# Sharing between two engines the scale that releases a store, and interleaving the tiles' rows in HBM, in a row-normalising kernel

## The chip, the cores and the metric

One core of one Trainium2 chip. The metric is device time in microseconds (us) of one execution.

## The reference

```python
x = np.random.randn(1024, 4096).astype(np.float32)      # eps = 1e-12
norm = np.sqrt(np.sum(x ** 2, axis=-1, keepdims=True) + eps)
return (x / norm).astype(np.float32)
```

16.78 MB are read, as many are written, and each element is squared once and scaled once.

## The kernel before

Two tiles of 128 partitions with four rows each. Both loads are issued at once; each store waits for all scales of its tile. Each row gets a sum of squares, a square root with a reciprocal (`norm`), and a scale.

```python
    def scale(self, r):                       # VectorE
        self.nc.vector.tensor_scalar_mul(
            out=self.x[:, r], in0=self.x[:, r], scalar1=self.rstd[:, r : r + 1])

    def scale_act(self, r):                   # ScalarE
        self.nc.scalar.activation(
            out=self.x[:, r], in_=self.x[:, r],
            func=ACT_F.Copy, scale=self.rstd[:, r : r + 1])
...
    x_t = x.rearrange("(t p r) d -> t p (r d)", p=P, r=R)           # P = 128, R = 4
    out_t = out_flat.rearrange("(t p r) d -> t p (r d)", p=P, r=R)
...
    for i, g in enumerate(groups):            # all loads are issued before this loop
        g.square_dve(R - 1)
        g.square_act(0); g.norm(0); g.scale(0)
        g.square_act(1); g.norm(1); g.norm(R - 1)
        g.scale(1); g.scale(R - 1)
        g.square_act(2); g.norm(2)
        if i < n_tiles - 1:
            g.scale_act(2)                    # the last scale of the first tile
        else:
            g.scale(2)
        store = nc.sync.dma_start(out=out_t[i], in_=g.flat())
```

## Time and profile before

| | before |
|---|---|
| time, median of the first 3 runs | 82.42 us (82.16 to 82.43) |
| profiled span | 80.7 us |
| DMA engines busy | 97.0% of the span |
| ScalarE, VectorE busy | 37%, 33% |
| loads landed at | 21.87 and 41.23 us |
| stores issued at | 39.21 and 56.61 us |
| stores landed at | 60.78 and 80.15 us |

The rows on landings and issues say it in short: four transfers of 8.39 MB follow each other at about 19.3 us apiece, and the compute lies beside them. The first store's own waits are in the view of the waits of the DMA queue's issuer (who waits, for what, us in total, times, longest; SPq is the queue of SyncE, which issues the DMAs, ACT is ScalarE and DVE is VectorE):

```profile
SPq L213 <- DMA xt<-in_x_dram: 22.4, 2, 20.7
SPq L213 <- ACT xt L69: 17.3, 1, 17.3
SPq L213 <- DVE xt L64: 15.3, 1, 15.3
```

The 17.3 us are the first store's wait for ScalarE's scale (L69) after the first load had landed. The last row, 15.3 us, is the second store's wait for VectorE's scale; it ends 3.4 us before the first engine has room for that store.

### The profile page before, as it was taken

The numbers are of one execution on the slowest core, as the hardware profiler recorded it, in microseconds if no ns is written. First come the engines' busy times: TensorE is split into PE (matmuls) and PEld (weight loads), VectorE is DVE, ScalarE is ACT, GpSimd is POOL, SyncE is SP. The second block draws the span as 40 slices with busy tenths as digits, with TensorE's granted clock in tenths as the row PEclk, the third lists the DMA queues.
The fourth block names the chain that finished last, engine by engine and source line by source line (L and its number), as shares of the span: only waits on it lengthen the run. The fifth ranks groups of instructions, "written<-read, shape, count | busy, mean of one in ns | idle before, by whom it ended". The sixth has DMA issues, their size and how long they took to land.

```text
span 80.7 us, 93 instructions
## 1 busy us (share of the span) xinstructions
DVE 26.2 (33%) x20; ACT 30.1 (37%) x23; POOL 0.2 (0%) x4
## 2 busy tenths in 40 slices
DVE  0000000000199599920059986999000000000000
ACT  6000000000199999989459999930000000000000
POOL 0000000000000000000000000000000000000000
DMA  9099998299998299998399992999993999993990
GB/s 520 0 520 520 520 520 390 130 520 520 520 520 390 130 520 520 520 520 390 130 520 520 520 520 130 390 520 520 520 520 130 390 520 520 520 520 130 390 520 0
DMA packets 576, 33.55 MB, mean 416 GB/s; under 512 B 64, under 2 KB 64, under 8 KB 64
## 3 DMA queue, kind: packets, MB, share of 16 engines
q1 hardware_dynamic: 576, 33.55, 97.0%
HBM read 16.78 MB, written 16.78 MB: 416 GB/s over the span
## 4 chain that ended last, share of the span: by engine, by line
DMA 50%; ACT 10%; DVE 9%; issue 0%
DMA xt<-in_x_dram 50%; ACT sq_act L33 9%; DVE xt L64 9%; ACT rstd L53 1%; DVE rstd L59 0%
## 5 line engine op out<-in xcount | busy, mean ns | idle before, releaser
L33 ACT ACTIVATE sq_act<-xt 128x4096 f32<-128x4096 f32 x6 | 21.6, 3608 | 21.9 <-DMA xt<-in_x_dram 21.9
L42 DVE SCALAR_TENSOR_TENSOR sq_dve<-xt 128x4096 f32<-128x4096 f32 x2 | 8.8, 4425 | 26.8 <-DMA xt<-in_x_dram 26.8
L64 DVE TENSOR_SCALAR xt<-xt,rstd 128x4096 f32<-128x4096 f32 x7 | 16.5, 2353 | 0.2
L69 ACT ACTIVATE xt<-xt,rstd 128x4096 f32<-128x4096 f32 x1 | 3.7, 3708 | 0.2 <-DVE rstd L59 0.2
L53 ACT ACTIVATE rstd<-ssq,eps_t 128x1 f32<-128x1 f32 x8 | 2.1, 288 | 0.1
L59 DVE RECIPROCAL rstd<-rstd 128x1 f32<-128x1 f32 x8 | 1.3, 159 | 2.4 <-ACT rstd L53 2.4
L33 ACT ACT_TABLE_LOAD x1 | 1.3, 1283 | 0.8 <-PEq L231 0.8
L53 ACT ACT_TABLE_LOAD x1 | 1.3, 1283 | 0.0
L33 ACT ACTIVATION_READ_ACCUMULATOR sq_act<-xt 128x1 f32 x6 | 1.1, 185 | 0.0
L184 DVE MEMSET eps_t<- 128x1 f32 x1 | 0.1, 59 | 0.9 <-PEq L231 0.9
L42 DVE DVE_READ_ACCUMULATOR sq_dve<-xt 128x1 f32 x2 | 0.2, 82 | 0.0
L231 POOL MEMSET const-bfloat16-1.0<- 128x1 bf16 x1 | 0.1, 101 | 0.0
L231 POOL MEMSET const-uint8-127<- 128x1 uint8 x1 | 0.1, 101 | 0.0
L231 POOL MEMSET const-float32-0.0<- 128x1 f32 x1 | 0.1, 98 | 0.2 <-issue 0.2
L231 POOL MEMSET const-float32-1.0<- 128x1 f32 x1 | 0.1, 98 | 0.0
## 6 DMA issues: line engine op xcount, KB each, us to landing
xt<-in_x_dram SPq DMA_DIRECT2D x2, 31.2
out_dram<-xt SPq DMA_DIRECT2D x2, 22.6
```

What stands on the lines that cost most here:

```text
L33: self.nc.scalar.activation(out=sq_a, in_=self.x[:, r], func=ACT_F.Square, accum_out=self.ssq[:, r : r + 1],)
L42: self.nc.vector.scalar_tensor_tensor(out=sq_v, in0=self.x[:, r], scalar=1.0, in1=self.x[:, r], op0=ALU.mult, op1=ALU.mult, accum_out=self ...
L53: self.nc.scalar.activation(out=self.rstd[:, r : r + n], in_=self.ssq[:, r : r + n], func=ACT_F.Sqrt, bias=self.eps_t,)
L59: self.nc.vector.reciprocal(out=self.rstd[:, r : r + n], in_=self.rstd[:, r : r + n])
L64: self.nc.vector.tensor_scalar_mul(out=self.x[:, r], in0=self.x[:, r], scalar1=self.rstd[:, r : r + 1])
L69: self.nc.scalar.activation(out=self.x[:, r], in_=self.x[:, r], func=ACT_F.Copy, scale=self.rstd[:, r : r + 1],)
L184: nc.vector.memset(eps_t, eps)
L231: nc = _bacc.Bacc("TRN2", target_bir_lowering=False, num_devices=1)
```

## The change

The intent is to release the first store sooner and to change how the tiles lie in HBM. ScalarE keeps 3072 of the 4096 elements of that scale and VectorE, idle at that time, takes 1024. Partition p of tile t now holds chunk 2p+t of four rows, so that the chunks of neighbouring partitions in one tile start 128 KiB apart in HBM instead of 64.

```diff
-    def scale_act(self, r):
+    def scale_by_both(self, r):
+        cut = 3 * self.D // 4
+        rstd = self.rstd[:, r : r + 1]
         self.nc.scalar.activation(
-            out=self.x[:, r], in_=self.x[:, r], func=ACT_F.Copy,
-            scale=self.rstd[:, r : r + 1])
+            out=self.x[:, r, :cut], in_=self.x[:, r, :cut], func=ACT_F.Copy,
+            scale=rstd)
+        self.nc.vector.tensor_scalar_mul(
+            out=self.x[:, r, cut:], in0=self.x[:, r, cut:], scalar1=rstd)
...
-    x_t = x.rearrange("(t p r) d -> t p (r d)", p=P, r=R)
-    out_t = out_flat.rearrange("(t p r) d -> t p (r d)", p=P, r=R)
+    x_t = x.rearrange("(p t r) d -> t p (r d)", t=n_tiles, r=R)
+    out_t = out_flat.rearrange("(p t r) d -> t p (r d)", t=n_tiles, r=R)
...
-            g.scale_act(2)
+            g.scale_by_both(2)
```

More of the change, by code (lines that the diff above doesn't have):

```diff
@@ L66, in scale @@
         )
-    def scale_act(self, r):
+    def scale_by_both(self, r):
+        cut = 3 * self.D // 4
+        rstd = self.rstd[:, r : r + 1]
         self.nc.scalar.activation(
-            out=self.x[:, r],
-            in_=self.x[:, r],
+            out=self.x[:, r, :cut],
+            in_=self.x[:, r, :cut],
             func=ACT_F.Copy,
-            scale=self.rstd[:, r : r + 1],
+            scale=rstd,
+        )
+        self.nc.vector.tensor_scalar_mul(
+            out=self.x[:, r, cut:], in0=self.x[:, r, cut:], scalar1=rstd
         )
```

## The prediction

> **What bounds the kernel now.** I began with the page of the profile: the busy shares, then the slices of DMA, then the chain.
>
> ```profile
> DVE 26.2 (33%) x20; ACT 30.1 (37%) x23; POOL 0.2 (0%) x4
> ...
> DMA  9099998299998299998399992999993999993990
> ...
> DMA packets 576, 33.55 MB, mean 416 GB/s; under 512 B 64, under 2 KB 64, under 8 KB 64
> ...
> q1 hardware_dynamic: 576, 33.55, 97.0%
> ```
>
> No compute engine is busy for even 40% of the span, while the 16 DMA engines are busy for 97.0% of it. The 0 and the 2s among the nines are no holes: all 16 engines move 64 KB packets nearly in step, and a slice's figure depends on which packets it catches. So I asked for longer stretches (columns: stretch, its length, busy time of three engines, clock, DMA share, GB/s):
>
> ```profile
> 0.00:18.00 18.00, 0.06 (x1) 1.28 (x1) 0.20 (x4) 1.00 0.98 408
> 18.00:40.00 22.00, 11.96 (x9) 16.97 (x12) 0.00 (x0) 1.00 0.99 429
> 40.00:43.00 3.00, 1.75 (x1) 1.75 (x1) 0.00 (x0) 1.00 0.87 371
> 43.00:60.00 17.00, 12.48 (x10) 10.12 (x10) 0.00 (x0) 1.00 1.01 436
> 60.00:80.70 20.70, 0.00 (x0) 0.00 (x0) 0.00 (x0) 1.00 0.92 399
> ```
>
> The stretch from 40 to 43 us, where the loads end and the first store begins, is the one soft spot inside the run. What releases that store is in the timeline (start, length, engine, line, operation):
>
> ```profile
> 34.95 0.29 ACT L53 ACTIVATE rstd<-ssq,eps_t 128x1 f32<-128x1 f32 x1
> 35.28 0.16 DVE L59 RECIPROCAL rstd<-rstd 128x1 f32<-128x1 f32 x1 [0.56 <-ACT rstd L53]
> 35.48 3.71 ACT L69 ACTIVATE xt<-xt,rstd 128x4096 f32<-128x4096 f32 x1 [0.23 <-DVE rstd L59]
> 39.21 17.74 SPq L213 DMA_DIRECT2D out_dram<-xt  x2
> 41.25 3.62 ACT L33 ACTIVATE sq_act<-xt 128x4096 f32<-128x4096 f32 x1 [2.06 <-DMA xt<-in_x_dram]
> 41.25 4.43 DVE L42 SCALAR_TENSOR_TENSOR sq_dve<-xt 128x4096 f32<-128x4096 f32 x1 [5.81 <-DMA xt<-in_x_dram]
> ...
> 54.23 2.35 DVE L64 TENSOR_SCALAR xt<-xt,rstd 128x4096 f32<-128x4096 f32 x1
> ```
>
> The scale that the change touches runs from 35.48 to 39.19 us, and the store is issued 0.02 us later, at 39.21. The second store of the merged row is issued when the last VectorE scale ends at 56.58. The chain of waits ends there as well and misleads: its shares add up to 69% of 80.7 us, because what follows, 24 us of stores, is nobody's wait.
>
> The packet records of the trace settle the size of the soft spot. There are 512 packets of 64 KB, 32 on each engine. The first 16 start at 1.02 to 1.68 us (mean 1.22) and end at a mean of 4.38. All later load packets take 2.418 to 2.42 us, store packets about 2.422. From the first load to the second the gap between packets on an engine is 0.002 us, and the same from the first store to the second. From the last load packet to the first store packet the mean end is 40.61 and the mean start 40.79: **a gap of 0.18 us**, where the engines have nothing to do.
>
> The run is thus 4.38 + 31 x 2.42 + 0.18 = 79.58 us; the records have a mean last end of 79.56, the last landing at 80.15 and the end of the span at 80.70. The kernel is bound by the pace of the DMA engines.
>
> **What the Trainium skill says.** "DMA: Bandwidth & Descriptors", section "Where 436 GB/s comes from", gives a ceiling of 435.2 GB/s for the 16 ports on the SBUF side. The trace has 16 x 65,536 B / 2.418 us = 433.7 GB/s, so it agrees: there is no rate left for a better layout to win.
>
> The same page, section "Latency and other measured facts", warns of row pitches in HBM at large powers of two: in its copies between HBM tensors a pitch of 512 KiB between partitions still gave 207 GB/s against 214 for a padded one, 2 MiB gave 164. Here each partition's row in a tile is 16,384 x 4 B = 64 KiB, packed; after the change the pitch is 128 KiB. That is below the pitch at which the page still has nearly full rate. No trace here has a pitch of 128 KiB.
>
> "ScalarE: Activation LUTs", section "What ACT_TABLE_LOAD costs", gives 0.833 ns an element, 186 ns with immediates and about 93 ns more for a per-partition pointer. For the scale: 279 + 4096 x 0.833 = 3691 ns; the trace has 3708. "VectorE: DVE Perf Modes", section "Mode 2×_2P", has two results a cycle for fp32 with a scalar operand; at the page's 0.96 GHz that makes 4096 / 1.92 = 2133 ns. The trace has 2353, so about 220 ns (an estimate) are fixed.
>
> **The change part by part.** First, the shared scale. The ScalarE piece shrinks to 3072 elements: an estimate of 3.708 - 1024 x 0.000833 = 2.855 us. It starts at 35.48 still, since nothing ahead of it changes, and ends at 38.33; the store is issued at about 38.35, **0.86 us earlier**. The VectorE piece of 1024 elements costs an estimated 0.220 + 1024 / 1920 = 0.75 us. The instruction order puts it directly behind the reciprocal that it needs, so it runs from 35.47 to 36.22 us in the 5.81 us in which VectorE idles before the second tile. The store now waits for VectorE too, but that wait is over 2.1 us before ScalarE's. Nothing else moves: tile two waits for its load, which lands at 41.23 either way.
>
> What are 0.86 us worth? Only what the DMA engines were idle. The first load needed 1.02 us from issue to its first packet and 1.68 us to its last engine's; I take the same for the store. Before: 39.21 + 1.02 = 40.23 to 39.21 + 1.68 = 40.89, against load packets that end from 40.33 to 40.92, so descriptors come about when the engines need them, or just too late. After: 38.35 + 1.68 = 40.03, all there before the first engine is free at 40.33. The gap should fall from 0.18 to 0.00 us. Every later packet moves up by that and no more: **-0.18 us**. The second store is issued at 56.6; the first engine would want it at 59.96 - 0.18 = 59.78, so 3.2 us remain against the 1.7 it needs.
>
> Second, the layout. Bytes, descriptors, 64 KiB runs and the partitions they land in stay the same; only HBM addresses differ. With packets at the port's pace in all 31 later rounds, I expect 0 us. The first round takes 3.16 us instead of 2.42, 0.74 too many; if that is a first access that depends on addresses, the layout could move part of it, either way. I take 0 with a doubt of 0.3 us.
>
> Sum: -0.18 + 0 = -0.18 us, profiled span 80.7 to 80.5. The three times of before are 82.16, 82.42 and 82.43, mean 82.34; 82.34 - 0.18 = 82.16, rounded to 82.2.
>
> **The rivals.** *The gap stays.* It may be the price of turning an engine from loading to storing, not of a late descriptor. For it: the gap is there on all 16 engines, 0.10 to 0.25 us, and even the first estimated arrival (40.23) is ahead of the first free engine (40.33). Against it: this is the only change of transfer whose issue came so late, 1.12 us ahead of the need, where the second store had 3.36 us and no gap. But that one is store after store, so the trace of before cannot part the two. I give it 35%; time unchanged, 82.3.
>
> *The layout costs.* Sixteen engines at twice the distance could meet in the same part of HBM. For it: the page's warning, and that they move in step. Against it: the pitch is small and the runs long. To lose 2%, 1.65 us, each of 32 rounds must take 0.05 us more, 2.47 in place of 2.42. I give 4% to a loss that large; the time would be 84 or more.
>
> *A large gain.* If the time followed the scale, all 0.86 us would come through, 81.5 us, 1.0%. Against it: the load packets run without a pause until 40.92 whatever the store does. Even without the gap and the slow first round, the gain would be 0.18 + 0.74 = 0.92 us, 1.1%. So 2% is out of reach unless packets get faster than the 2.418 us, for which nothing speaks. I give it 1%.
>
> **Range and chances.** The middle is 82.2. Low: 0.18 from the gap, 0.2 of the first round and the noise of the runs (0.27 us from lowest to highest) together reach about 81.8. High: no gain, a little loss from the layout and the noise reach about 82.6. Faster by over 2%: 0.01; within: 0.95; slower: 0.04.
>
> **What would show it.** Right: the shared scale at about 2.86 us on ScalarE and 0.75 on VectorE; the store issued near 38.35; from the last load to the first store no gap above 0.01 us; packets still 2.42; the last landing near 79.97. If the gap is still 0.1 us or more with the store issued at 38.35, the reversal of direction is its cause and my step from descriptors fails. If packets take over 2.45 us, or the first round's end leaves 4.38 by over 0.3 us, the layout matters and my zero is wrong. If the store is issued later than 38.6, the instruction cost was mis-sized.

## The result, and the profile after

After: 82.28 us median of 6 runs (82.20 to 82.42); before, in the same rounds and the three earlier runs: 82.49 us (82.16 to 82.71). The ratio is 0.9977, interval 0.9953 to 1.0001: 0.2 us, within 2%. Ratios here are the mean time of one kernel's fast runs over that of the other's of the same rounds, so not quite the ratio of the medians quoted.

The page of the changed kernel, its lines on busy time, DMA and queues:

```profile
DVE 27.0 (34%) x21; ACT 29.3 (36%) x23; POOL 0.2 (0%) x4
...
DMA  9099999399999399999399999399999399998390
...
q1 hardware_dynamic: 576, 33.55, 97.0%
```

About 0.8 us of work moved from ScalarE to VectorE, and the DMA engines are as busy as before. The page's rows of instructions have the two pieces of the scale (mean ns after the bar):

```profile
L72 ACT ACTIVATE xt<-xt,rstd 128x3072 f32<-128x3072 f32 x1 | 2.9, 2858 | 0.2 <-DVE rstd L59 0.2
L78 DVE TENSOR_SCALAR xt<-xt,rstd 128x1024 f32<-128x1024 f32 x1 | 0.8, 753 | 0.0
```

The timeline of the changed kernel around the first store:

```profile
35.58 2.86 ACT L72 ACTIVATE xt<-xt,rstd 128x3072 f32<-128x3072 f32 x1 [0.23 <-DVE rstd L59]
35.58 0.75 DVE L78 TENSOR_SCALAR xt<-xt,rstd 128x1024 f32<-128x1024 f32 x1
38.46 18.55 SPq L219 DMA_DIRECT2D out_dram<-xt  x2
41.31 3.62 ACT L33 ACTIVATE sq_act<-xt 128x4096 f32<-128x4096 f32 x1 [2.88 <-DMA xt<-in_x_dram]
```

Both pieces start together, VectorE's is done 2.1 us before ScalarE's, and the store goes out at 38.46. The second tile still starts when its load lands, at 41.31. The issuer's waits say the same:

```profile
SPq L219 <- DVE xt L78: 35.2, 1, 35.2
...
SPq L219 <- ACT xt L72: 2.1, 1, 2.1
```

The first wait was written down to VectorE because the queue met it first; the one that counts is the 2.1 us for ScalarE after it.

One stretch of the windows needs care. This is 40 to 43 us of the changed kernel:

```profile
40.00:43.00 3.00, 1.69 (x1) 1.69 (x1) 0.00 (x0) 1.00 1.26 546
```

A DMA share of 1.26 and 546 GB/s are more than the packets' own pace gives (433.7 GB/s). A stretch of 3 us holds little more than one round of 2.42 us packets, and its figure depends on how the rounds fall in it. The prediction read the 371 GB/s of before in that stretch as a soft spot. That reading was worth nothing by itself; only the packet records carried it.

The packet records, sorted by start and taken as 32 rounds of 16 (one packet an engine), are the basis of all that follows. Rounds 1 to 16 are loads, 17 to 32 stores. "Gap" is the mean start of round 17 less the mean end of round 16. "Stretch" is how much longer than 2.418 us the packets of round 16, the last loads, took. The records do not name the engine of a packet, so "the last engine" and any gap of a single engine are taken from the order in time.

| packet records | before | after |
|---|---|---|
| end of round 1, mean, us | 4.377 | 4.346 |
| stretch, mean, ns | 2 | 11 |
| gap, us | 0.178 | 0.002 |
| store packets, mean, ns | 2426.1 | 2418.5 |
| end of round 32, mean / last engine, us | 79.563 / 79.804 | 79.235 / 79.582 |

The gap is gone, 0.176 us. Store packets became 7.6 ns shorter, in 16 rounds 0.122 us. The first round ended 0.031 us sooner, and the stretch takes 0.009 back. That is 0.32 us of the 0.328 by which the mean end moved. The kernel ends with its last engine, however, and that one gained 0.222 us, about as much as the span and the time. For it the parts differ: its own gap was only 0.097 us before and is 0.003 after, its 16 store packets took 38.785 us before and 38.637 after, and its last load ended 0.020 us later. So on the engine that ends the kernel the shorter store packets gave 0.148 us and the closed gap 0.094.

### The profile page after: what moved, and what is told of

Read it like the earlier page. It is cut to its first block, busy times and chain, and to the rows that moved or that the text cites. A ratio compares the mean times of both kernels' runs of the same rounds, so it can differ in the third digit from the quotient of the medians.

```text
span 80.5 us, 94 instructions
## 1 busy us (share of the span) xinstructions
DVE 27.0 (34%) x21; ACT 29.3 (36%) x23; POOL 0.2 (0%) x4
## 4 chain that ended last, share of the span: by engine, by line
DMA 50%; ACT 10%; DVE 9%; issue 0%
DMA xt<-in_x_dram 50%; ACT sq_act L33 9%; DVE xt L64 9%; ACT rstd L53 1%; DVE rstd L59 0%
## 5 line engine op out<-in xcount | busy, mean ns | idle before, releaser
L72 ACT ACTIVATE xt<-xt,rstd 128x3072 f32<-128x3072 f32 x1 | 2.9, 2858 | 0.2 <-DVE rstd L59 0.2
L78 DVE TENSOR_SCALAR xt<-xt,rstd 128x1024 f32<-128x1024 f32 x1 | 0.8, 753 | 0.0
```

Of the source, the lines that this page charges most:

```text
L72: self.nc.scalar.activation(out=self.x[:, r, :cut], in_=self.x[:, r, :cut], func=ACT_F.Copy, scale=rstd,)
L78: self.nc.vector.tensor_scalar_mul(out=self.x[:, r, cut:], in0=self.x[:, r, cut:], scalar1=rstd)
```

## The experiments

Two theories at first: the descriptors of the store, the orders that tell each engine what to move, came too late ("late descriptor"), or the gap is the price of turning an engine from loads to stores; beside them the question which part of the change did it. Kernels are compared only within the same rounds.

**The shared scale alone.** The layout lines are put back.

```diff
-    x_t = x.rearrange("(p t r) d -> t p (r d)", t=n_tiles, r=R)    # out_t likewise
+    x_t = x.rearrange("(t p r) d -> t p (r d)", p=P, r=R)
```

> The shared scale alone, with the old layout. Theory 'late descriptor': the store is issued near 38.4 us and the mean gap from the last load packet to the first store packet falls from 0.18 to under 0.01 us; time 0.2 us below before (ratio 0.9975). Rival 'layout': the gap closed because of the new HBM addresses, so here it stays at 0.15 us or more and the time is that of before (ratio 1.000).

Measured: 82.64 us, ratio 1.0006 (0.9985 to 1.0027). The gap fell to 0.003 us as the theory said, and no gain shows. The timeline of this kernel shows the loss:

```profile
38.36 0.35 SPq L219 DMA_DIRECT2D out_dram<-xt  x1
41.78 3.62 ACT L33 ACTIVATE sq_act<-xt 128x4096 f32<-128x4096 f32 x1 [3.45 <-DMA xt<-in_x_dram]
```

The second load landed near 41.76 instead of 41.23. In the packet records the last load packets took 129 ns longer on the mean, one of them 627 ns. Neither theory had this: in this profile the load ahead of the earlier store was slower. Whether the early issue did it is tested below.

**The layout alone.** The scale stays whole on ScalarE.

```diff
-    x_t = x.rearrange("(t p r) d -> t p (r d)", p=P, r=R)          # out_t likewise
+    x_t = x.rearrange("(p t r) d -> t p (r d)", t=n_tiles, r=R)
```

> The new layout alone, with the whole scale on ScalarE. Theory 'late descriptor': store issued near 39.2 us, gap 0.15 to 0.2 us as before, time as before (ratio 1.000, within 0.1%). Rival 'layout': gap under 0.01 us and ratio 0.9975. A part effect of the layout would show in the store packets: 2.418 us each instead of 2.422 would be 0.06 us in all over 16 rounds.

Measured: 82.50 us, ratio 0.9998 (0.9982 to 1.0014); gap 0.181 us; store packets 2425.8 ns. The layout by itself is worth nothing, and it is not what made the store packets shorter.

**The whole change again**, on the chip of the two parts (no edit).

> The whole change once more on this chip, as the yardstick for the two parts: ratio 0.9975, gap under 0.01 us. If the parts add up, the savings of the shared scale alone and of the layout alone sum to this one within 0.1 us.

Measured: 82.25 us, ratio 0.9975 (0.9955 to 0.9994); gap 0.002 us, stretch 13 ns. The parts do not add up in these runs: +0.05 and -0.02 us alone, by the ratios, and -0.2 together; but the intervals of the shared scale alone and of the whole change still overlap (0.9985 to 0.9994).

**The store later.** ScalarE copies 1024 elements of the scaled row onto themselves.

```diff
             scale=self.rstd[:, r : r + 1],
         )
+        self.nc.scalar.activation(
+            out=self.x[:, r, :1024], in_=self.x[:, r, :1024], func=ACT_F.Copy
+        )
```

> The old kernel with one more ScalarE instruction behind the scale, which copies 1024 of its elements onto themselves (result still right), so that the store is issued about 1.05 us later, at 40.27. Theory 'late descriptor': before was at the edge, so nearly the whole delay reaches the gap: 0.18 + 1.05 = 1.23 us, time 1.05 us longer (83.4, ratio 1.013). Rival 'price of the reversal': the gap of 0.18 us is fixed and descriptors had some slack, so less than 0.9 us are added.

Measured: 82.87 us, ratio 1.0037 (1.0022 to 1.0052), 0.3 us and not 1.05. Timeline of this kernel:

```profile
39.35 1.06 ACT L75 ACTIVATE xt<-xt 128x1024 f32<-128x1024 f32 x1
40.43 0.35 SPq L216 DMA_DIRECT2D out_dram<-xt  x1
```

The store's packets start 0.85 to 1.00 us after the issue on all 16 engines, at 41.28 to 41.43. Here the queue was empty or nearly so, so this is what a store needs from its issue. Applied to before, 39.21 + 1.00 = 40.21, which is ahead of the first free engine at 40.33. By that measure the descriptors of before were not late, unless a busy engine takes up a descriptor more slowly than an idle one, which no run here can tell from a price of the turn. The mean gap grew to 0.77 us, but the last engine's only from 0.097 to 0.462, because a common late start evens the engines out: they start within 0.15 us instead of 0.49.

**The store a little later.** The same with 384 elements.

> As the late store, but with a copy of 384 elements: store issued about 0.52 us later than before, at 39.73. 'Late descriptor': gap 0.18 + 0.52 = 0.70 us and 0.5 us longer (ratio 1.006). 'Price of the reversal': gap well below 0.6 us.

Measured: 82.51 us, ratio 1.0012 (0.9995 to 1.0028). Issued at 39.77, 0.56 us later than before; gap 0.226 us, only 0.05 more. So there is a plateau of about 0.2 us. The engine that became free last, at 40.84, found its store 0.07 us old at least (39.77 + 1.00 = 40.77) and still stood idle for 0.21 us. On this reading the rival is right that far: turning from loads to stores has a price.

**The store a little earlier.** Old layout, ScalarE keeps 3584 elements.

```diff
-        cut = 3 * self.D // 4        # with the old layout
+        cut = 7 * self.D // 8
```

> Old layout, ScalarE keeps 3584 of 4096 elements: store issued 0.43 us earlier than before, near 38.78. 'Late descriptor' with 1.02 us to the first engine and 1.68 to the last: all are there before the engines are free (40.46 for the last against 40.9), gap under 0.01 us, and the whole gain (ratio 0.9975) is had already. If descriptors need more time than I took from the first load, some gap is left.

Measured: 82.17 us, ratio 0.9962 (0.9947 to 0.9977), the lowest of all; issued at 38.85, gap 0.015 us, stretch 8 ns, store packets 2418.8 ns. Timeline:

```profile
35.55 3.28 ACT L72 ACTIVATE xt<-xt,rstd 128x3584 f32<-128x3584 f32 x1 [0.23 <-DVE rstd L59]
38.85 0.35 SPq L219 DMA_DIRECT2D out_dram<-xt  x1
```

Half the shift, and no new layout, has the whole gain. So if the turn has a price, it is not fixed: here an issue 0.36 us earlier hides it.

**The store much earlier.** Old layout, the scale halved.

```diff
-        cut = 3 * self.D // 4        # with the old layout
+        cut = self.D // 2
```

> Old layout, scale halved between the engines: ScalarE 2.00 us, VectorE 1.29, store issued 1.7 us earlier than before, near 37.5. Theory: no further gain over the cut at 3072, gap under 0.01 us, ratio 0.9975. Rival 'the time follows the scale': 0.85 us more than with the cut at 3072 (ratio 0.987).

Measured: 83.14 us, ratio 1.0081 (1.0064 to 1.0098), slower than before by 0.7 us. Timeline:

```profile
35.59 2.00 ACT L72 ACTIVATE xt<-xt,rstd 128x2048 f32<-128x2048 f32 x1 [0.23 <-DVE rstd L59]
35.59 1.29 DVE L78 TENSOR_SCALAR xt<-xt,rstd 128x2048 f32<-128x2048 f32 x1
37.62 0.35 SPq L219 DMA_DIRECT2D out_dram<-xt  x1
42.13 3.62 ACT L33 ACTIVATE sq_act<-xt 128x4096 f32<-128x4096 f32 x1 [4.53 <-DMA xt<-in_x_dram]
```

The store goes out 1.6 us sooner than before, and the second load lands 0.9 us later. All 16 last load packets are stretched, by 650 to 942 ns, mean 794. No gap, and the first store packets are not shorter for it (2.418 us), so the time is lost.

**No compute at all.** The loop holds only the stores. Its output is wrong, which doesn't matter for the time.

```diff
-        g.square_dve(R - 1)
-        ...                          # every square, norm and scale
         store = nc.sync.dma_start(out=out_t[i], in_=g.flat())
```

> Wrong result on purpose: both loads and both stores, no compute at all. It is the floor of this DMA plan. Theory: loads and stores still follow each other on the queue, 32 packets an engine at 2.42 us and a first round of 3.1 to 3.2, no gap: time as with the change, 82.1 to 82.3 (ratio 0.9975). Rival: the compute engines slow the packets, so this is over 0.5 us faster than the changed kernel.

Measured: 83.52 us, ratio 1.0128 (1.0113 to 1.0143). I had called it the floor, and it is slower than the kernel with all its compute by 1.1 us. Its timeline:

```profile
21.77 21.12 SPq L198 DMA_DIRECT2D out_dram<-xt  x2
```

The store is issued at 21.77, 19 us before its turn. The last load packets are stretched by 1.29 us on the mean; the mean of every other round after the first lies between 2418 and 2424 ns. Nothing computes on the tiles here, so compute is not the cause of this stretch. The second store, too, was issued 18.4 to 19.0 us ahead of the first store's last packets, and those stayed at 2.418 us: the load ahead of an early store was stretched, the store ahead of one was not.

**Old layout, the cut at 3200** (`cut = 3200`).

> Old layout, ScalarE keeps 3200 elements, so the store is issued about 0.11 us later than with the shared scale alone, near 38.47, as late as in the changed kernel. Theory 'issue time alone': the stretch of the last load packets (mean 128 ns with the shared scale alone) falls to about 15 ns and the time is that of the changed kernel, 82.25 (ratio 0.997). Theory 'layout shelters': with the old addresses some packets are still stretched, mean over 60 ns, and the time stays near 82.5.

Measured: 82.36 us, ratio 0.9983 (0.9957 to 1.0009); issued at 38.63 and not 38.47, as this profile ran 0.15 us late from the first load on; stretch 11 ns, gap 0.002 us. No packet is stretched by more than 16 ns in the old layout either when the store is issued 0.27 us later than in the first run with the shared scale alone.

**New layout, the cut at 2944** (`cut = 2944`).

> New layout, ScalarE keeps 2944 elements, so the store is issued about 0.11 us earlier than in the changed kernel, near 38.33, as early as with the shared scale alone in the old layout. 'Issue time alone': the last load packets are stretched by over 100 ns on the mean, time near 82.6 (ratio 1.001). 'Layout shelters': stretch under 30 ns, time 82.25 (ratio 0.997).

Measured: 82.23 us, ratio 0.9978 (0.9955 to 1.0001); issued at 38.18, stretch 59 ns on the mean and 175 at most. It lies between the two expectations: stretched with the new layout too, but by less.

**New layout, the scale halved** (`cut = 2048`).

> New layout, scale halved, store issued near 37.6. 'Issue time alone': the last load packets are stretched by about 0.79 us as in the old layout, time 83.1 (ratio 1.008). 'Layout shelters': stretch under 0.3 us and time below 82.6.

Measured: 82.94 us, ratio 1.0051 (1.0032 to 1.0071); issued at 37.45, stretch 695 ns. The layout does not shelter.

**The shared scale alone, again** (no edit).

> The shared scale alone, once more, on this chip. If its loss is real: 82.5 to 82.7 again with last load packets stretched by about 100 ns on the mean and one by over 0.4 us. If it was chance: 82.25 and a stretch of about 15 ns.

Measured: 82.36 us, ratio 0.9984 (0.9963 to 1.0006); issued at 38.48, stretch 22 ns on the mean, one packet 231 ns. Between the expectations. The loss of the first time was real in its profile but is not the rule.

All profiles in the order of their lead. "Lead" is the time from the store's issue to the moment at which an engine would have ended its last load packet at 2.418 us, smallest to largest of the 16 engines:

| kernel | layout | lead, us | gap, us | stretch mean (max), ns | ratio |
|---|---|---|---|---|---|
| 1024 copied, later | old | -0.25 to 0.54 | 0.771 | 1 (4) | 1.0037 |
| 384 copied, later | old | 0.54 to 1.07 | 0.226 | 1 (4) | 1.0012 |
| before | old | 1.12 to 1.70 | 0.178 | 2 (14) | 1 |
| layout alone | new | 1.16 to 1.64 | 0.181 | 1 (4) | 0.9998 |
| cut 3584 | old | 1.47 to 2.04 | 0.015 | 8 (16) | 0.9962 |
| cut 3200 | old | 1.57 to 2.38 | 0.002 | 11 (16) | 0.9983 |
| cut 3072, second run | old | 1.74 to 2.47 | 0.002 | 22 (231) | 0.9984 |
| cut 3072, first run | old | 1.80 to 2.48 | 0.003 | 129 (627) | 1.0006 |
| the change | new | 1.92 to 2.47 | 0.002 | 11 (16) | 0.9977 |
| the change, again | new | 1.97 to 2.49 | 0.002 | 13 (43) | 0.9975 |
| cut 2944 | new | 2.04 to 2.59 | 0.002 | 59 (175) | 0.9978 |
| cut 2048 | old | 2.71 to 3.33 | 0.003 | 794 (942) | 1.0081 |
| cut 2048 | new | 2.89 to 3.34 | 0.002 | 695 (1048) | 1.0051 |
| no compute | old | about 19 | 0.002 | 1291 (1544) | 1.0128 |

Read from top to bottom: too late and the engines idle, too early and the last loads drag. Between a lead of 1.5 and 2.4 us neither costs much in most profiles.

These are no thresholds, for the lead does not decide it engine by engine. The five engines of before with leads of 1.47 to 1.70 us idled 0.10 to 0.20 us; of the 12 engines of the cut at 3584 with leads in the same range, ten idled no more than 0.013. And in the first run of the cut at 3072 ten of the 16 last load packets, at leads of 1.80 to 2.48, were stretched by 48 to 627 ns, while none of the change's, at 1.92 to 2.47, was stretched by more than 16. What else decides, no run here shows.

## Why the prediction was right or wrong

**Time.** 82.28 us against 82.2 and a range of 81.8 to 82.6; within 2%, as forecast at 0.95.

**The shared scale.** Right: 2.858 us against 2.855, 0.753 against 0.75. The store was issued 38.46 - 35.58 = 2.88 us after the scale's start, against 3.73 before; the whole profile had moved on by 0.1 us. VectorE's wait ended 2.1 us before ScalarE's, as said. The last landing, forecast near 79.97, was at 79.93.

**What the earlier issue is worth.** The rule, that only the engines' idle time can be won, held in part: of 0.85 us, 0.176 closed the mean gap, and the rest had no gap left to close. The predicted -0.18 meets the measured -0.21 in part by luck. A term was missing: store packets became 7.6 ns shorter, 0.122 us in all. The prediction read them as "about 2.422", which is near the median of before (2.423); the mean is 2.426, because the first store round took 2.454 us and the eighth 2.443. The others, those of the second store too, took 2.421 to 2.427, so it is no price paid once at the turn. Over both stores the packets take 2425.8 to 2427.2 ns on the mean in the four profiles with a gap of 0.18 us or more and 2418.0 to 2418.8 in all others, in both layouts, so this goes with the gap and not with the layout. And the mean of the engines was the wrong thing to add: the last engine gained 0.222 us, not 0.328, and only 0.094 of it is the gap that the prediction counted.

**"So descriptors come about when the engines need them, or just too late."** This step failed. I took 1.02 to 1.68 us from the first load; an idle queue needed 0.85 to 1.00 for the store. Had before been at the edge, a store 0.56 us later would have added about as much to the gap; it added 0.05. The gap closed as I had said, but not for the reason that I gave. The plateau at 0.2 us between leads of 0.5 and 1.7 speaks for a price of the turn from loads to stores, which was my rival's claim at 35%. The rival's conclusion, that the gap stays, failed as well. What the runs show in place of both is a gap of about 0.2 us that an issue 0.36 us earlier (38.85 against 39.21, mean gap 0.015) all but hides. How the engine hides it, and whether it lies in fetching the descriptor or in moving the first bytes, no run shows.

**The layout, 0 us.** Right for the layout alone (0.9998), and in the changed kernel the load packets of rounds 2 to 15 took 2.418 to 2.420 us at a pitch of 128 KiB. Whether it helps beside the shared scale is open. On one chip the shared scale alone was at 82.64 us and the whole change at 82.25; on another the shared scale alone was at 82.36, and at 82.23 a new-layout kernel with an even earlier store. The stretch near a lead of 2.5 us tended to be smaller with the new layout, and also at 3 us (695 against 794 ns), but with one profile each this is a hint. By the means of the runs the new-layout kernel was ahead by 0.28 us on the first chip and by 0.05 on the other.

**"A large gain" rejected.** Right: issuing another 0.8 us sooner made the kernel slower. But the prediction had no thought of that; it took early issue for harmless, with load packets that "run without a pause until 40.92 whatever the store does". With the cut at 2048 in the old layout they ran until 41.81. That the change landed in the narrow stretch that pays was not foreseen.

**A better version.** The cut at 3584 with the old layout had the lowest ratio, 0.9962 against 0.9977 and 0.9975 for the change. The intervals overlap and the chips differ, so it is not shown to beat the change. It gets the same with one part of it.

## What to carry to other kernels

When DMA bounds a kernel, a shorter wait before a store wins little more than the time in which the DMA engines idle: here 0.85 us of earlier issue won 0.2. The packet records show that time while short stretches of GB/s do not. When loads are followed by stores on one queue, issue the store neither late nor as early as possible: in this one kernel 1.5 to 2.4 us ahead of the last load's end was best, one profile excepted, and 19 us ahead made the kernel 1.1 us slower than before. Sum up the engine that ends last, not the mean of them, and do not take a kernel without compute for a floor.

## What the Trainium skill lacked or had wrong

- "DMA: Bandwidth & Descriptors", section "Rules for kernel authors", advises to issue a DMA early so that its fixed setup cost overlaps. No run contradicts it for a load behind a load (gap 0.002 us with the second load issued at 0.79 us) or a store behind a store (lead 2.5 to 4.2 us, and 18.4 to 19.0 in the kernel without compute, last packets of the first store 2.418 us). For a store behind loads it cost: last load packets 0.70 to 0.79 us longer at a lead of 3 us, 1.29 us longer at 19.
- The same page has nothing on the turn from loads to stores: a gap of 0.18 to 0.23 us an engine at leads of 0.5 to 1.7 us, and store packets of 2426 instead of 2418 ns after it.
- The same page, section "Latency and other measured facts", gives about 600 ns to the first byte for DMAs issued from the sync queue. Here the first store packets started 0.85 to 1.00 us after the issue on engines that were idle or just becoming so; the two need not be counted from the same event.
- The row pitch of that section starts at 512 KiB. These runs add one below: at 128 KiB, the changed kernel's load packets of rounds 2 to 15 took 2.4188 us on the mean, before's at 64 KiB 2.4191.
